# The order of 512- and 256-column matmuls inside the wide block products of two gated FFNs

## The chip, the cores and the metric

The kernel is one program on one core of a Trainium2 chip. The metric is the device time of one execution in microseconds (us), taken as the median over several runs. Matrix products run on TensorE (PE in the profile; its weight loads stand in a row of their own, PEld), sums and evacuations on VectorE (DVE), copies and activations on ScalarE (ACT), a few sums and some DMA issues on GpSimd (POOL), and most loads are issued by SyncE (SP).

## The reference, cut to what matters

The kernel computes a two-layer decoder trunk over 512 tokens of width 1024 in float32. Each layer adds a mixer to the residual stream and then a gated feed-forward network (FFN) of inner width 2816; a final norm ends it. The change touches the two FFNs alone:

```
def gated_conv_ffn(x, w_gate, w_up, conv_w, conv_b, w_down):
    g = jnp.einsum('bsd,df->bsf', x, w_gate)
    g = causal_dwconv3(g, conv_w) + conv_b
    up = jnp.einsum('bsd,df->bsf', x, w_up)
    return jnp.einsum('bsf,fd->bsd', jax.nn.silu(g) * up, w_down)
...
    hn = rms_norm(h, norm_ffn[layer])
    h = h + gated_conv_ffn(hn, w_ffn_gate[layer], w_ffn_up[layer], ...)
```

## The kernel before, in words

**Split floats.** TensorE multiplies in a format that keeps only part of a float32, so every operand is split into a high part (`hi`, a rounded copy made by ACT) and a low part (`lo`, the remainder, made by DVE or by an accumulating DMA that POOL issues). A product is then hi·hi + hi·lo + lo·hi. In most of the kernel this is three matmuls per 128 rows of the contraction (`mm3`, L157 to L159): the same high weights against the high and the low moving operand, then the low weights against the high moving operand.

**FFN by units.** The 22 blocks of 128 inner columns are worked off in units of two, `f` = 0, 2, ... 20, once in each layer. Unit 0 is computed directly. Each of the other ten is a fast block product (seven half-size products in place of eight) for the gate (`g`) and for the up projection (`u`): 14 products a unit, in the order written in `Ffn.products`. Each product contracts 512 rows, that is `NP` = 4 steps `kp`, with stationary weights of 128 columns and half the tokens (`HALF` = 256) as the moving operand. Between the units stand the down projections (`d` in layer 0, `dn` in layer 1) through `mm3`, long runs of 512-column matmuls.

**One block product** is the function `multiply` (L558 to L583). It has two forms:

- Narrow (`both` is None, L577 to L583): for each `kp` three 256-column matmuls into the first half of one PSUM bank.
- Wide (`both` given, L569 to L576): the tiles of the moving operand hold hi and lo side by side, so one 512-column matmul takes the high weights against both (hi·hi into columns 0 to 255 of the bank, hi·lo into columns 256 to 511), and a 256-column matmul adds lo·hi onto the first half. The wide form first runs the four 512-column matmuls of `kp` = 0 to 3 (L571), then the four 256-column ones (L574). `start` is set only on the first matmul into a freshly opened bank, so the order of the others doesn't matter to the sum. DVE adds both halves of the bank afterwards (`add`, L804).

`in_both` chooses the form: all products of units 6 to 20 are wide; in unit 4 all seven of the gate and three of the up projection are; in unit 2 none is.

**What sets the order.** A scheduler orders the instructions of each engine, with the program's order as its guide; tiles come from rotating pools (`whi` and `wlo`, six buffers each; seven PSUM banks `mm`), and a tile's next writer waits for its last reader. Some instructions are tied to others by hand (`behind`, `inorder`). The last matmul that `multiply` issues is kept in `last_matmul` and is what the fetch of the second layer's parameters is tied behind.

**Weights of a unit** (`prepare`): four loads by SP, then sums (`s12`, `s34`) on DVE and splits on ACT with DVE or with POOL's accumulating DMA. Names in the profile: `whi_a`/`wlo_a`, `whi_s12g`, `wlo_s34u` and so on; `g_20b` is a PSUM bank of unit 20's gate.

Of the kernel before, what the change touches and what calls it, by code (L numbers as in the profile page):

```python
# [31 lines left out]
def tile_trunk(ctx: ExitStack, tc: tile.TileContext, x, norm_mix, norm_ffn, final_norm,  # L32
# [13 lines left out]
    def mm_bank(name):  # L46
        return ps_mm.tile([P, 512], F32, tag="mm", name=name)
# [501 lines left out]
    NP = NK // 2  # L549
# [8 lines left out]
    def multiply(banks, name, product, left, right, both=None):  # L558

        at = BANK[product]
        first = at not in banks
        if first:
            banks[at] = mm_bank(f"{name}{at}")
        ps = banks[at][:, :HALF]
        if both is not None:  # L569
            for kp in range(NP):  # L570
                nc.tensor.matmul(banks[at], left(kp)[0], both(kp), start=first and kp == 0,  # L571
                                 stop=kp == NP - 1, skip_group_check=True)
            for kp in range(NP):
                last_matmul[0] = nc.tensor.matmul(ps, left(kp)[1], right(kp)[0], start=False,  # L574
                                                  stop=kp == NP - 1, skip_group_check=True)
            return banks[at]  # L576
        for kp in range(NP):  # L577
            (a_hi, a_lo), (b_hi, b_lo) = left(kp), right(kp)
            for l, r, end in ((a_hi, b_hi, False), (a_hi, b_lo, False),
                              (a_lo, b_hi, kp == NP - 1)):  # L580
                nc.tensor.matmul(ps, l, r, start=first, stop=end, skip_group_check=True)  # L581
                first = False
        return ps  # L583
# [8 lines left out]
    class Ffn:  # L592
# [127 lines left out]
        def multiply(self, banks, name, product, weights_, both):  # L720
            hi, lo = weights_
            return multiply(banks, name, product, lambda kp: (hi[:, kp, :], lo[:, kp, :]),
                            lambda kp: self.moving(product, kp),
                            (lambda kp: self.moving_both(product, kp)) if both else None)
# [173 lines left out]
    def mixer1(norm):  # L898
        w = w_in_odd[0]
        with tc.tile_pool(name="m1", bufs=1) as mp:  # L900
# [72 lines left out]
            class InProducts:  # L973
# [31 lines left out]
                def run(self, out_, done, behind_first):  # L1005
                    banks = ({}, {})
                    e = {}
                    for i, product in ((0, 1), (1, 1), (0, 2), (1, 2), (0, 6), (1, 6), (0, 5),
                                       (0, 7), (1, 5), (1, 7), (0, 4), (0, 3), (1, 4), (1, 3)):
                        if (i, product) == (0, 2):  # L1010
                            behind_first()
                        hi, lo = self.stat[product]
                        ps = multiply(banks[i], f"{self.name}_{i}", product, tokens(product, i),
                                      lambda kp: (hi[:, kp, :], lo[:, kp, :]))
                        c = {1: (0, 0), 2: (0, 0), 6: (0, 1), 3: (0, 1), 7: (1, 1), 5: (1, 1),
                             4: (1, 0)}[product]
                        dst = out_(i + 2 * c[0])[:, c[1] * HALF : (c[1] + 1) * HALF]
                        if product in (1, 6):
                            nc.scalar.copy(dst, ps)
                        elif product == 5:  # L1020
                            e[i] = ps
                        elif product == 7:
                            nc.scalar.copy(dst, ps)
                            nc.vector.tensor_tensor(dst, e[i], dst, ALU.add)
                            gelu(dst, dst, i + 2)
                        elif product == 4:
                            gelu(dst, ps, i + 2)
                            done(i + 2)
                        else:
                            nc.vector.tensor_tensor(dst, ps, dst, ALU.add)  # L1030
                        if product == 3:
                            row = out_(i)
                            gelu(row, row, i)
                            done(i)
# [398 lines left out]
```

## Time and profile before

| | |
|---|---|
| median of 3 runs (lowest to highest) | 975.62 us (975.47 to 975.7) |
| span of the profiled execution, first to last instruction | 973.0 us |
| PE busy | 963.6 us, 99%, 5120 matmuls |
| DVE busy | 817.0 us, 84% |
| ACT busy | 598.7 us, 62% |
| 512-column matmuls of the wide products (L571) | 976 |
| 256-column matmuls of the wide products (L574) | 976 |
| 256-column matmuls of the narrow products (L581) | 768 |

The profile is of one execution. Its own device time is not listed apart from its span; the span and the median differ by 2.6 us. A matmul's row carries its start, its modelled duration, its line and its tiles (`out<-in`, then the shape of the output). Matmuls overlap in the rows: the next one starts long before the duration of the one before has ended, so the pace is read from the distance of the starts. The timeline merges neighbours of the same line and tiles into one row (x4): the first start, and the time from it to the end of the last. Since matmuls overlap in the rows, the busy share of PE says little here.

### The profile page before, as it was taken

How to read it: one execution, taken by the hardware profiler on the slowest of the kernel's cores; microseconds unless marked ns; L12 is line 12 of the kernel's file. 1: busy time of each engine (PE TensorE's matmuls, PEld its weight loads, DVE VectorE, ACT ScalarE, POOL GpSimd, SP SyncE). 2: the span in 40 equal slices, each digit the busy share in tenths (PEclk: the TensorE clock that was granted, in tenths of full speed). 3: DMA queues.
4: the chain of work that ended last, by engine and by line, in shares of the span. 5: the costliest groups of instructions: out<-in, count | busy, mean ns of one | idle time of the engine just before them, and what ended most of it. 6: DMA issues, size and time to landing. Idle time of an engine off the chain costs nothing.

```text
span 973.0 us, 14003 instructions
## 1 busy us (share of the span) xinstructions
PE 963.6 (99%) x5120; PEld 828.8 (85%) x5120; DVE 817.0 (84%) x1393; ACT 598.7 (62%) x905; POOL 149.9 (15%) x173
## 2 busy tenths in 40 slices
PE   9999999999999999999999999999999999999996
PEld 7888888988888888888889988889888888888885
DVE  5887458999899898998986865589998989889897
ACT  5523347765676665765487734587765667656775
POOL 2142023110111010110310001221111011100123
PEclk9999999999999999999999999999999999999999
DMA  7442225776777677774324623167767777668775
GB/s 251 146 139 86 87 88 108 178 178 165 195 178 181 146 178 185 174 174 140 119 58 110 221 67 99 55 132 187 186 145 194 196 173 172 156 165 201 194 153 140
DMA packets 94417, 148.36 MB, mean 152 GB/s; under 512 B 5156, under 2 KB 60428, under 8 KB 94348
## 3 DMA queue, kind: packets, MB, share of 16 engines
q1 hardware_dynamic: 78316, 98.69, 32.2%
q0 software_dynamic: 14256, 46.93, 26.7%
q10 hardware_dynamic: 1776, 1.84, 0.6%
q8 instruction: 40, 0.66, 0.3%
q14 instruction: 29, 0.24, 0.1%
HBM read 98.42 MB, written 2.10 MB: 103 GB/s over the span
## 4 chain that ended last, share of the span: by engine, by line
PE 99%; DVE 1%; issue 0%; ACT 0%; POOLq 0%; DVEq 0%; POOL 0%
PE dn L158 3%; PE d L158 3%; PE dn L159 3%; PE dn L157 3%; PE d L159 3%; PE d L157 3%; PE gu L157 2%; PE gu L159 2%; PE oo L159 1%; PE oo L157 1%; PE gu L158 1%; PE oe L157 1%; PE oe L159 1%; PE oo L158 1%; PE oe L158 1%; PE u_2a L581 1%
## 5 line engine op out<-in xcount | busy, mean ns | idle before, releaser
L617 DVE SCALAR_TENSOR_TENSOR c<-rows,prm,c 128x512 f32<-128x512 f32 x88 | 65.6, 748 | 1.5 <-ACT c L615 1.4
L144 POOL DMA_DIRECT2D wlo_g<-raw_g x20 | 17.2, 860 | 321.3 <-DVE kept L804 187.4
L158 PE MATMUL dn<-wlo_dn,a_hi 128*128 128x512 f32 x144 | 56.3, 391 | 0.0
L158 PE MATMUL d<-a_lo,whi_d 128*128 128x512 f32 x144 | 56.3, 391 | 0.0
L159 PE MATMUL dn<-whi_dn,a_lo 128*128 128x512 f32 x144 | 56.2, 391 | 0.0
L159 PE MATMUL d<-a_hi,wlo_d 128*128 128x512 f32 x144 | 56.2, 390 | 0.0
L157 PE MATMUL d<-a_hi,whi_d 128*128 128x512 f32 x144 | 56.2, 390 | 0.0
L157 PE MATMUL dn<-whi_dn,a_hi 128*128 128x512 f32 x144 | 56.2, 390 | 0.0
L731 ACT ACTIVATE whi_a<-raw_g 128x512 fp32r<-128x512 f32 x20 | 12.6, 631 | 61.0 <-PE g_10e L571 8.7
L213 POOL TENSOR_TENSOR ssq_f<-ssq_f,sq_f 128x512 f32<-128x512 f32 x14 | 19.8, 1411 | 134.4 <-ACT sq_f L212 99.5
L202 ACT ACTIVATE hg<-h,prm 128x512 fp32r<-128x512 f32 x24 | 17.3, 722 | 34.9 <-DVE h L315 34.9
L142 ACT ACTIVATE wlo_g<-raw_g 128x1024 fp32r<-128x1024 f32 x20 | 21.2, 1062 | 27.5 <-PE g_2e L581 8.8
L615 ACT ACTIVATE c<-rows,prm 128x512 f32<-128x512 f32 x44 | 31.3, 715 | 6.6 <-DVE rows L828 6.6
L1187 DVE SCALAR_TENSOR_TENSOR y<-dn,small,y 128x512 f32<-128x512 f32 x40 | 28.0, 749 | 8.6 <-PE dn L159 8.6
L625 ACT ACTIVATE s<-c,prm 128x512 f32<-128x512 f32 x44 | 31.4, 715 | 6.2 <-DVE c L617 6.1
L203 DVE SCALAR_TENSOR_TENSOR hg<-h,prm,hg 128x512 fp32r<-128x512 f32 x24 | 23.6, 986 | 11.1 <-ACT hg L202 11.1
L266 ACT ACTIVATE a_hi<-s 128x512 fp32r<-128x512 f32 x40 | 24.9, 627 | 11.4 <-PE d L159 7.7
L159 PEld LDWEIGHTS dn<-whi_dn,a_lo 128*128 128x128 f32 x144 | 27.1, 188 | 5.7
L159 PEld LDWEIGHTS d<-a_hi,wlo_d 128*128 128x128 f32 x144 | 27.1, 188 | 5.6
L153 DVE TENSOR_TENSOR wlo_dn<-raw_dn,whi_dn 128x1024 fp32r<-128x1024 f32 x18 | 22.0, 1224 | 11.7 <-ACT whi_dn L152 11.7
L157 PEld LDWEIGHTS dn<-whi_dn,a_hi 128*128 128x128 f32 x144 | 27.1, 188 | 5.3
L157 PEld LDWEIGHTS d<-a_hi,whi_d 128*128 128x128 f32 x144 | 27.1, 188 | 5.3
(1132 smaller groups left out, 3319.9 us busy)
## 6 DMA issues: line engine op xcount, KB each, us to landing
raw_g<-in_w_ffn_gate_dram SPq DMA_DIRECT2D x40, 512.0 KB, 3.8
raw_u<-in_w_ffn_up_dram SPq DMA_DIRECT2D x40, 512.0 KB, 4.0
raw_dn<-in_w_ffn_down_dram SPq DMA_DIRECT2D x22, 512.0 KB, 6.3
wlo_u<-raw_u POOLq DMA_DIRECT2D x21, 512.0 KB, 6.1
wlo_g<-raw_g POOLq DMA_DIRECT2D x20, 512.0 KB, 4.6
raw_d<-in_w_ffn_down_dram SPq DMA_DIRECT2D x18, 512.0 KB, 4.2
wlo_s12g<-s12g POOLq DMA_DIRECT2D x18, 512.0 KB, 6.3
wlo_s34g<-s34g POOLq DMA_DIRECT2D x18, 512.0 KB, 5.5
```

The lines of the kernel that those rows point to most:

```text
L142: first = nc.scalar.activation(lo, raw, AF.Copy, scale=-1.0)
L153: behind(nc.vector.tensor_tensor(lo, raw, hi.bitcast(F32), ALU.subtract), after[0])
L157: nc.tensor.matmul(ps, lhs[0], rhs[0], start=start, stop=False)
L158: nc.tensor.matmul(ps, lhs[0], rhs[1], start=False, stop=False)
L159: nc.tensor.matmul(ps, lhs[1], rhs[0], start=False, stop=stop)
L203: nc.vector.scalar_tensor_tensor(hg[k][1], h[k], g, hg[k][0].bitcast(F32), op0=ALU.mult, op1=ALU.subtract)
L213: nc.gpsimd.tensor_tensor(self.ssq, self.ssq, sq, ALU.add)
L266: nc.scalar.activation(hi, src, AF.Copy, scale=scale)
L615: nc.scalar.activation(c, t[:, 0:S], AF.Copy, scale=prm("cf", ft))
L617: self.last_conv = nc.vector.scalar_tensor_tensor(c, t[:, i : S + i], prm("cf", i * NF + ft), c, op0=ALU.mult, op1=ALU.add)
L625: self.last_silu = nc.scalar.activation(s, c, AF.Silu, bias=self.prm("bf", ft))
L1187: return nc.vector.scalar_tensor_tensor(dst, ps, ffn.cols[:, t : t + 1], dst, op0=ALU.mult, op1=ALU.add)
```

## The change

In the wide form, the second loop over `kp` goes: each 512-column matmul is followed at once by the 256-column matmul of the same `kp`. The number of instructions, their operands and shapes, the `start` and `stop` marks and the bank stay as they were.

```diff
         if both is not None:
             for kp in range(NP):
                 nc.tensor.matmul(banks[at], left(kp)[0], both(kp), start=first and kp == 0,
                                  stop=kp == NP - 1, skip_group_check=True)
-            for kp in range(NP):
                 last_matmul[0] = nc.tensor.matmul(ps, left(kp)[1], right(kp)[0], start=False,
                                                   stop=kp == NP - 1, skip_group_check=True)
             return banks[at]
```

The order of the built instructions, set beside that of before: on PE 732 of the 976 matmuls of L574 move (the fourth of each product stays last); the order of POOL and SP is the same in both; on DVE and ACT the scheduler exchanges neighbours in some units. In six products (`u_6b` of both layers, `u_8b`, `u_10b`, `u_14b` and `u_18b` of layer 0) it lets another product in between, before as after.

## The prediction

> **What bounds the kernel now.** I read the profile's page first, for the shares of the engines and the chain that ended last, then the waits of PE, then PE's timeline in the units that the change touches.
>
> ```profile
> span 973.0 us, 14003 instructions
> ...
> PE 963.6 (99%) x5120; PEld 828.8 (85%) x5120; DVE 817.0 (84%) x1393; ACT 598.7 (62%) x905; POOL 149.9 (15%) x173
> ...
> PEclk9999999999999999999999999999999999999999
> ...
> PE 99%; DVE 1%; issue 0%; ACT 0%; POOLq 0%; DVEq 0%; POOL 0%
> ```
>
> The chain is PE from end to end, at full granted clock. A busy PE could still be a waiting one, so the waits (line that waited <- who ended it: total us, times, longest):
>
> ```profile
> PE clock L61 <- DVE idle L56: 1.3, 1, 1.3
> PE z L441 <- ACT hg L409: 0.3, 1, 0.3
> ```
> ```profile
> PEld g_10a L571 <- DVE rows L804: 0.3, 1, 0.3
> ```
>
> In the FFNs PE's weight loader waits 0.3 us once, and nothing else. So what counts is the pace of the matmul stream itself: the distance from one start to the next. The change alters no instruction; it alters only which matmul stands next to which. How many are touched, from the stage sums taken by line over the whole span (busy us, count):
>
> ```profile
> 0.00:974.00 974.00, 266.15 (x976) 168.51 (x976) 1.00 0.60 152
> ```
> ```profile
> 0.00:974.00 974.00, 155.14 (x976) 149.55 (x976) 1.00 0.60 152
> ```
>
> The first is L571, the 512-column matmul (W below), the second L574, the 256-column one (N): 976 each, that is 244 wide products of WWWWNNNN, which become WNWNWNWN. 1 ns on a pair is 0.98 us on the kernel.
>
> **The paces that the trace shows.** Long runs of one size first: the down projection behind the last unit (all 512 columns), and unit 2 (all 256; each x2 row counts two):
>
> ```profile
> 937.87 0.39 PE L158 MATMUL dn<-wlo_dn,a_hi 128*128 128x512 f32 x1
> ...
> 945.58 0.39 PE L159 MATMUL dn<-whi_dn,a_lo 128*128 128x512 f32 x1
> ```
> ```profile
> 173.77 0.40 PE L581 MATMUL g_2a<-t,whi_s12g 128*128 128x256 f32 x2
> ...
> 185.29 0.40 PE L581 MATMUL g_2a<-t,whi_g 128*128 128x256 f32 x2
> ```
>
> The first fence spans 34 matmuls: 7.71 / 34 = 0.2268 us for a settled W. The second spans 8 products of 12: 11.52 / 96 = 0.1200 us for a settled N. A wide product at settled paces would be 4 x 0.2268 + 4 x 0.1200 = 1.387 us. Now the wide products themselves, first to last of unit 20, with the run of 512s that follows:
>
> ```profile
> 916.64 1.09 PE L571 MATMUL u_20a<-hg,whi_a 128*128 128x512 f32 x4
> 917.57 0.63 PE L574 MATMUL u_20a<-hg,wlo_a 128*128 128x256 f32 x4
> 918.04 1.09 PE L571 MATMUL g_20b<-hg,whi_g 128*128 128x512 f32 x4
> 918.97 0.64 PE L574 MATMUL g_20b<-hg,wlo_g 128*128 128x256 f32 x4
> ...
> 934.88 0.40 PE L157 MATMUL dn<-whi_dn,a_hi 128*128 128x512 f32 x1
> 935.11 0.40 PE L158 MATMUL dn<-wlo_dn,a_hi 128*128 128x512 f32 x1
> 935.35 0.40 PE L159 MATMUL dn<-whi_dn,a_lo 128*128 128x512 f32 x1
> 935.58 0.39 PE L157 MATMUL dn<-whi_dn,a_hi 128*128 128x512 f32 x1
> ```
>
> Thirteen products from 916.64 to 934.88: 18.24 / 13 = **1.403 us each**, 16 ns over the settled sum. Four W take 0.93 (0.2325 each, slower than settled), four N 0.47 (0.1175 each, faster than settled). And after N's, the W's of the down projection start 0.23 to 0.24 apart (935.11 to 935.58 is 0.47 for two) before they settle. So a W that follows N's is slower than one that follows many W's. The opposite case, a wide product right behind a run of 512s:
>
> ```profile
> 193.64 1.07 PE L571 MATMUL g_4a<-hg,whi_a 128*128 128x512 f32 x4
> ...
> 194.54 0.64 PE L574 MATMUL g_4a<-hg,wlo_a 128*128 128x256 f32 x4
> ```
>
> Four W in 0.90: settled pace. Hence neither the split moving tile nor the switch of line makes a W slow; what came before does.
>
> **The change part by part.** Nothing is removed or added; the terms are the W after an N and the N after a W, now four of each per product in place of one. Single matmuls in ns come from the rows of a line (count: min/median/max duration):
>
> ```profile
> L571 PE MATMUL g_4a<-hg,whi_a x8: 389/390/390, 193.6 to 676.9; 128*128 128x512 f32 x8
> ```
> ```profile
> L571 PE MATMUL g_4b<-hg,whi_g x1: 396/396/396, 196.5 to 196.5; 128*128 128x512 f32 x1
> ```
> ```profile
> L581 PE MATMUL u_4a<-hg,wlo_a x1: 284/284/284, 196.3 to 196.3; 128*128 128x256 f32 x1
> ```
> ```profile
> L571 PE MATMUL g_20b<-hg,whi_g x1: 396/396/396, 918.0 to 918.0; 128*128 128x512 f32 x1
> ```
> ```profile
> L574 PE MATMUL u_20a<-hg,wlo_a x2: 278/278/279, 917.8 to 917.9; 128*128 128x256 f32 x2
> ```
> ```profile
> L574 PE MATMUL g_4a<-hg,wlo_a x8: 278/283/284, 194.5 to 677.5; 128*128 128x256 f32 x8
> ```
>
> A duration is about 163 ns longer than the distance to the next start (390 in g_4a at a settled 226.8; 284 at the end of the narrow u_4a at a settled 120). The border of g_4b: the N before it 284 - 163 = 121, its first W 396 - 163 = 233, together 354. The border of g_20b: 278 - 163 = 115 and 233, together 348. I take the mean, **351 ns for a pair**, because it is the only place where the trace has an N and a W side by side in that order; the ends 348 and 354 are kept. A product becomes 4 x 0.351 = 1.404 against 1.403: +1 ns, x 244 = +0.2 us, with -2.7 us and +3.2 us at the ends (1.392 and 1.416).
>
> What moves with it: the first N of a product is now second in place of fifth, so its low weights are wanted three W's (0.70 us) earlier. The tightest that I found:
>
> ```profile
> 222.14 1.22 DVE L732 TENSOR_TENSOR wlo_s12u<-s12u,whi_s12u 128x1024 fp32r<-128x1024 f32 x1
> ```
> ```profile
> 225.38 0.28 PE L574 MATMUL u_6e<-t,wlo_s12u 128*128 128x256 f32 x1
> ```
>
> Written by 223.36, read at 225.38, then at about 224.7: 1.3 us are left; 0. The high weights are free later: the fourth W starts 3 x 0.351 = 1.05 us into the product, not 0.70. ACT waits for these buffers:
>
> ```profile
> ACT whi_a L731 <- PE g_10e L571: 8.7, 2, 4.5
> ```
>
> 4.5 us become about 4.9, on an engine that is idle 38% of the time: 0; if that cover were gone, twice 0.35 us in each of 18 units or 12.6 us, which bounds it. The product's last matmul, and with it the bank's evacuation, keeps its place. On DVE some neighbours change places, and DVE is close to full in these units:
>
> ```profile
> 320.00:500.00 180.00, 180.00 (x915) 153.38 (x914) 164.92 (x285) 111.38 (x159) 24.82 (x24) 1.00 0.60 152
> ```
>
> 164.92 / 180 = 92% of DVE. An add that frees a bank may come behind a 1.22 us split. I take two more waits of the size of the one listed (0.3 us), 0.6 us, and keep 18 of them, 5.4 us, as the upper end and 0 as the lower. DMAs keep their order on SP and POOL, so no transfer moves past another. **Sum:** +0.2 + 0.6 = +0.8 us on the span of 973.0; the span lies 2.6 us under the median of 975.62, and nothing touched lies outside it, so 975.6 + 0.8 = 976.4, said as 976.5.
>
> **The Trainium skill** (page "TensorE: Matmul & The Clock Gate", section "Back-to-back issue gap") gives the isolated distance of matmuls as columns / 2.4 + 2.5 ns, 215.8 and 109.2 here; the trace has 226.8 and 120.0, 11 ns more, and the measurement decides. By that rule a matmul's time hangs on its own size alone, which is the first rival below.
>
> **The rivals.**
> 1. *Blind to order.* Each matmul costs its size whatever stands beside it: the change is nothing, 975.6. Against it: W at 0.225 in g_4a and 0.2325 elsewhere. 0.08.
> 2. *The switch has a fee (slower).* The 16 ns that a product pays over the settled sum are the price of one round from W to N and back; four rounds pay four times: 3 x 16 = 48 ns x 244 = +11.7 us, 987; three fees in place of four if part of it is shared, 984. It decides from 2 ns a round more than now. For it: the excess is there in every product behind another, and missing where a product follows 512s. Against it: it builds up over several W's (0.93 for four), so one W should pay a part. 0.20.
> 3. *Short runs never upset the pace (faster).* The slow W's come from a run of N's; a single N leaves the settled pace alone. Pair 226.8 + 120.0: 1.387, -16 ns x 244 = -3.9 us, 971.7; 0.16. If the lone N also keeps the short distance of the first N behind a settled run (278 - 163 = 115), 1.367: -8.8 us, 966.8; 0.05. Against it: at both borders above the very first W is slow already.
> 4. *Engines fall behind.* The exchanged adds on DVE make PE wait as in the upper end: +5.4 us, 981. Against it: one wait in 244 products today. 0.11.
>
> That the change doesn't do what it says is excluded but for six products, between whose matmuls the scheduler lets another product, as before.
>
> **How the numbers follow.** The forecast (pair at 348 to 354) has 0.40: 0.04 of it faster, 0.24 the same, 0.12 slower, by 0.2% or 1.95 us, about what a measurement of this kernel can tell from no change. Rival 1 adds 0.08 to the same, rival 2 0.20 to slower, rival 3 0.21 to faster, rival 4 0.09 to slower and 0.02 to the same. Faster 0.25, same 0.34, slower 0.41. The likeliest case alone gives 973 to 979. For 8 in 10 the range goes down to 971, which leaves out rival 3's second price, and up to 986, which leaves out the upper half of rival 2.
>
> **What would show it.** In the profile after, the rows of L571 and L574 stand singly, so each start can be read. A pair of 0.348 to 0.354 and products of 1.39 to 1.42 bear out the forecast; 0.347 or less is rival 3; 0.36 and more is rival 2. PE waits on DVE's L804 of over 2 us in total are rival 4. ACT's wait for L571 should grow by 0.35 us each, at no cost. Wrong I would be above all if an N alone between two W's sets a pace that no row of before shows.

## The result, and the profile after

| | before | after |
|---|---|---|
| median of 7 runs (lowest to highest) | 975.25 us (975.03 to 975.7) | 977.65 us (977.21 to 979.59) |
| span of the profiled execution | 973.0 us | 975.5 us |

The change costs 2.4 us: a ratio of 1.0029, with a 95% interval of 1.0018 to 1.004. That is slower by 0.2 to 0.3%. The forecast was 976.5, in a range of 971 to 986.

The page of the kernel after, its span, its engines and its chain:

```profile
span 975.5 us, 14004 instructions
...
PE 965.6 (99%) x5120; PEld 826.8 (85%) x5120; DVE 815.9 (84%) x1393; ACT 597.7 (61%) x905; POOL 150.4 (15%) x173
...
PE 97%; ACT 1%; DMA 1%; DVE 1%; issue 0%; POOLq 0%; DVEq 0%; POOL 0%
```

The busy shares say almost nothing. The chain says something: before, it was PE at 99% and DVE at 1%. DVE's 1%, the work at the end, is still there; new is that the chain leaves PE between 210 and 226 us, for ACT and then for one DMA. So there is a new wait. The waits of PE's weight loader in the kernel after (who waited, for whom: total us, times, longest; the lines of `multiply` and `add` have moved up by one, L573 for L574, L803 for L804):

```profile
PEld u_6b L573 <- DMA wlo_u<-raw_u: 0.7, 1, 0.7
...
PEld g_16a L571 <- DVE rows L803: 0.3, 2, 0.2
PEld g_12a L571 <- DVE rows L803: 0.3, 2, 0.2
```

**Where the time lies.** The stretch from the first wide product of a layer to the down projection behind the last unit holds all that the change touches. In layer 1, PE's timeline of after, then of before:

```profile
677.20 0.39 PE L571 MATMUL g_4a<-hg,whi_a 128*128 128x512 f32 x1
...
948.27 0.39 PE L1280 MATMUL dn_a<-whi_dnp,hg 128*128 128x512 f32 x1
```
```profile
676.25 0.62 PE L571 MATMUL g_4a<-hg,whi_a 128*128 128x512 f32 x2
...
945.80 0.39 PE L1281 MATMUL dn_a<-whi_dnp,hg 128*128 128x512 f32 x1
```

271.07 us against 269.55. The same was worked out for both layers and for two traces of each kernel (the second ones are the first and the ninth experiment). From the starts of all matmuls of the wide products I took the mean distance to the next start, W and N added to a pair. A W with more than 245 ns to the next start, or an N with more than 130, was counted as a wait, with what it has over 235 or 118 ns:

| | stretch, layer 0 / 1 (us) | pair (ns) | waits (us) |
|---|---|---|---|
| before | 269.75 / 269.55 | 350.17 / 350.28 | 0.26 / 0.00 |
| before, second trace | 270.19 / 269.55 | 350.15 / 350.28 | 0.72 / 0.00 |
| after | 271.56 / 271.08 | 352.25 / 351.63 | 1.08 / 0.90 |
| after, second trace | 271.47 / 271.58 | 352.13 / 352.44 | 1.03 / 0.89 |

Everything else in the program has kept its length, but for the start-up (the time to the first product of unit 2) and the mixer of the second layer, which differ by 0.8 and 0.6 us between the two traces of after as well. The start-up is why the two spans lie only 2.5 us apart: it took 167.24 us in the first trace of after, 168.02 in that of before. The stretches give +3.3 us in these traces (542.85 against 539.52 for both layers together, the means of two traces). Of this the pace is 1.9 ns x 976 = 1.85 us, and the waits are 1.95 - 0.5 = 1.45 us. **Two halves**, and either could be the whole in a theory; the experiments take them apart.

**The first new wait, one of 0.66 us.** PE's timeline of after, at the product that the scheduler splits:

```profile
225.13 0.28 PE L573 MATMUL u_6e<-t,wlo_s12u 128*128 128x256 f32 x1
225.25 0.40 PE L571 MATMUL u_6b<-hg,whi_u 128*128 128x512 f32 x1
226.04 0.39 PE L573 MATMUL u_6b<-hg,wlo_u 128*128 128x256 f32 x1 [0.40 <-DMA wlo_u<-raw_u]
226.27 0.39 PE L571 MATMUL u_6b<-hg,whi_u 128*128 128x512 f32 x1
```

The tile `wlo_u` of after (the DMA that makes it, its first and last start, then its time to landing), and before the first W's of `u_6b` and the N's that read the tile:

```profile
L144 POOL DMA_DIRECT2D wlo_u<-raw_u x1: 859/859/859, 218.3 to 218.3; - x1
...
DMA to landing us min/median/max: 7.7/7.7/7.7
```
```profile
225.86 0.86 PE L571 MATMUL u_6b<-hg,whi_u 128*128 128x512 f32 x3
```
```profile
L574 PE MATMUL u_6b<-hg,wlo_u x4: 281/282/284, 231.0 to 231.4; 128*128 128x256 f32 x4
```

The low weights land at 218.3 + 7.7 = 226.0. Before, they landed at 219.0 + 7.6 = 226.6, and the first of the N's stood at 231.0: the scheduler had let three whole products in between the first W of `u_6b` (225.86) and its N's. Now the first N is the second matmul of `u_6b`, due at 225.25 + 0.24 = 225.49.

**The other new waits, 18 of 0.01 to 0.10 us in the distances of starts, together 1.3.** They all stand at the first W of product 7 (on `s34g` or `s34u`), which writes the bank that product 6 has left to DVE. Unit 12 of layer 0, before: ACT, DVE, PE.

```profile
317.46 1.06 ACT L152 ACTIVATE whi_d<-raw_d 128x1024 fp32r<-128x1024 f32 x1 [0.55 <-PE g_12a L571]
318.42 0.35 ACT L816 COPY rows<-g_12a 128x256 f32<-128x256 f32 x1
```
```profile
318.55 1.23 DVE L153 TENSOR_TENSOR wlo_d<-raw_d,whi_d 128x1024 fp32r<-128x1024 f32 x1 [1.17 <-ACT whi_d L152]
319.69 0.42 DVE L804 TENSOR_TENSOR rows<-g_12a,rows 128x256 f32<-128x256 f32 x1
```
```profile
320.49 1.09 PE L571 MATMUL g_12a<-t,whi_s34g 128*128 128x512 f32 x4
```

And after, the same three engines:

```profile
318.05 1.06 ACT L152 ACTIVATE whi_d<-raw_d 128x1024 fp32r<-128x1024 f32 x1 [0.91 <-PE g_12a L571]
319.01 0.35 ACT L815 COPY rows<-g_12a 128x256 f32<-128x256 f32 x1
```
```profile
319.14 1.23 DVE L153 TENSOR_TENSOR wlo_d<-raw_d,whi_d 128x1024 fp32r<-128x1024 f32 x1 [1.16 <-ACT whi_d L152]
320.28 0.42 DVE L803 TENSOR_TENSOR rows<-g_12a,rows 128x256 f32<-128x256 f32 x1
```
```profile
320.63 0.28 PE L573 MATMUL u_12a<-t,wlo_s12u 128*128 128x256 f32 x1
320.76 0.50 PE L571 MATMUL g_12a<-t,whi_s34g 128*128 128x512 f32 x1
```

Read it as a chain. ACT's next instruction, the copy of the down projection's high weights (`whi_d`), needs the buffer that product 6's high weights leave, and these are read by the fourth W. The brackets show ACT's wait grown from 0.55 to 0.91 us. DVE's `wlo_d` needs `whi_d`, and behind it on DVE stands the add that frees the bank. The add starts 0.59 us later than before (320.28 for 319.69), while PE itself is only 0.27 us later (320.76 for 320.49). Before, the add had ended 0.38 us ahead of the W (319.69 + 0.42 = 320.11); now 0.06 us (320.70), and that is too little: the W's row is 0.50 long in place of 0.40, and the next start comes 0.33 us after its own.

### The profile page after: what moved, and what is told of

Read it like the earlier page. It is cut to its first block, busy times and chain, and to the rows that moved or that the text cites. A ratio compares the mean times of both kernels' runs of the same rounds, so it can differ in the third digit from the quotient of the medians.

```text
span 975.5 us, 14004 instructions
## 1 busy us (share of the span) xinstructions
PE 965.6 (99%) x5120; PEld 826.8 (85%) x5120; DVE 815.9 (84%) x1393; ACT 597.7 (61%) x905; POOL 150.4 (15%) x173
## 4 chain that ended last, share of the span: by engine, by line
PE 97%; ACT 1%; DMA 1%; DVE 1%; issue 0%; POOLq 0%; DVEq 0%; POOL 0%
PE dn L159 3%; PE dn L158 3%; PE dn L157 3%; PE d L157 3%; PE d L159 3%; PE d L158 3%; PE gu L157 2%; PE gu L159 1%; PE oo L159 1%; PE oo L158 1%; PE gu L158 1%; PE oe L159 1%; PE oe L157 1%; PE oo L157 1%; PE oe L158 1%; PE u_2a L580 1%
## 5 line engine op out<-in xcount | busy, mean ns | idle before, releaser
L730 ACT ACTIVATE whi_a<-raw_g 128x512 fp32r<-128x512 f32 x20 | 12.6, 632 | 62.0 <-PE g_8e L571 8.8
L158 PEld LDWEIGHTS dn<-wlo_dn,a_hi 128*128 128x128 f32 x144 | 27.1, 188 | 5.4
L158 PEld LDWEIGHTS d<-a_lo,whi_d 128*128 128x128 f32 x144 | 27.1, 188 | 5.3
```

Source lines behind the costliest of these rows:

```text
L158: nc.tensor.matmul(ps, lhs[0], rhs[1], start=False, stop=False)
```

## The experiments

**Theory A**: the two halves are separate and add up, a slower pace of the order 1+1 and waits that come from product 6's weights being freed late and from `u_6b`. **Rivals**: B, each switch between W and N has a fee of its own; C, the waits are all, and the slower pairs only their echo; D and E, on the pace, that it suffers only at the switches, or that the first two N's are cheap and the later ones dear. F, G and H came up later.

All kernels but those of e1 and e9, which are after and before unchanged, share one edit: the two lines in the loop become a loop over a string that gives the order of the product's matmuls (W and N, each in the order of `kp`).

```diff
+            for kind in ORDER:
+                kp, seen[kind] = seen[kind], seen[kind] + 1
...
```

Only ORDER is shown below; after is `"WNWNWNWN"`, before `"WWWWNNNN"`. Each time stands beside its own runs of before: 974.82 for the first four, 974.94 for the next four, 974.91 and 974.85 for the last two pairs.

| run | time (us) | ratio to before, 95% | stretch 0 / 1 (us) | pair (ns) | waits (us) |
|---|---|---|---|---|---|
| e1 after again | 977.99 | 1.0035 (1.0023 to 1.0048) | 271.47 / 271.58 | 352.13 / 352.44 | 1.03 / 0.89 |
| e2 product 6 grouped | 977.79 | 1.0032 (1.0021 to 1.0042) | 271.70 / 270.69 | 351.27 / 352.28 | 1.68 / 0.00 |
| e3 only product 6 split | 975.89 | 1.0011 (1.0002 to 1.002) | 269.95 / 270.38 | 349.74 / 349.73 | 0.65 / 1.13 |
| e4 2+2 | 972.92 | 0.9981 (0.9972 to 0.999) | 269.74 / 268.63 | 348.31 / 348.29 | 1.35 / 0.28 |
| e5 pace alone | 976.78 | 1.0017 (1.0008 to 1.0026) | 271.44 / 270.65 | 351.69 / 352.21 | 1.14 / 0.00 |
| e6 only `u_6b` grouped | 977.41 | 1.0022 (1.0013 to 1.0032) | 270.52 / 271.27 | 351.19 / 352.08 | 0.56 / 0.91 |
| e7 runs of eight | 973.39 | 0.9986 (0.9977 to 0.9995) | 270.03 / 268.65 | 349.14 / 349.10 | 1.33 / 0.00 |
| e8 2+2, three places 4+4 | 972.81 | 0.9979 (0.997 to 0.9987) | 269.59 / 268.52 | 348.47 / 348.45 | 1.08 / 0.00 |
| e9 before again | 975.39 | one run | 270.19 / 269.55 | 350.15 / 350.28 | 0.72 / 0.00 |
| e10 3+3, 1+1 | 975.78 | 1.0012 (1.0002 to 1.0021) | 270.25 / 270.45 | 350.25 / 350.20 | 0.77 / 1.02 |
| e11 1+1 with turned pairs | 978.76 | 1.0043 (1.0026 to 1.006) | 271.60 / 271.41 | 351.64 / 352.66 | 1.48 / 0.90 |
| e12 the same without waits | 975.19 | 1.0007 (0.9998 to 1.0017) | 269.73 / 270.15 | 350.48 / 351.58 | 0.23 / 0.20 |

**e1**, the kernel after once more, as the ground for the others.

> The changed kernel once more, beside the others of this group. Theory A (two halves: a pace of 352 ns a pair in place of 350.2, +1.75 us, and new waits of PE, +1.65 us, that come from high weights freed 0.35 us later and from low weights wanted earlier): +2 to +3 us, and the waits of the first profile stand at the same places (first W of product 7 behind unit 12, 16, 20; the second matmul of u_6b). Rival B (the switch between sizes has a fee, 0.8 us for each further round in a product; waits only take up what PE would lose elsewhere): +2 to +3 us, waits anywhere. Rival C (waits alone, no pace): +2 to +3 us, and the pairs that do not wait stand 350 ns apart.

It repeats the result: +3.2 us here, both halves as in the first trace.

**e2** gives product 6 its old order, so its high weights are free as early as before:

```diff
-ORDER = "WNWNWNWN"
+ORDER = "WWWWNNNN" if product == 6 else "WNWNWNWN"
```

> As changed, but product 6 of gate and up goes back to 4+4 (36 of 244 products), so that its high weights are freed early again. A: the waits before product 7 go (about -1.0 us) and 36 products get their pace back (-0.25 us): +1.1 to +1.5 us over before, and the first W of s34g and s34u takes 230 to 240 ns in every unit. B: 36/244 of 2.4 us less: +2.0 us. C: +1.4 us.

In layer 1 the waits go from 0.90 to 0.00, and what is left of the stretch, 270.69 - 269.55 = 1.14 us, is pace alone (352.28 - 350.28 = 2.0 ns x 488 pairs = 0.98). So the chain through product 6's weights is what makes those waits, and C falls: the pairs stay slow without a wait. The time hardly moved, +3.0 us over before where A had +1.1 to +1.5, since in this trace layer 0 lost elsewhere what it had gained. PE's loader in this run:

```profile
PEld u_6b L578 <- DMA wlo_u<-raw_u: 0.8, 1, 0.8
PEld u_10a L575 <- DVE kept L809: 0.7, 1, 0.7
```

**e3** is the mirror image, before with product 6 alone at 1+1:

```diff
-ORDER = "WWWWNNNN"
+ORDER = "WNWNWNWN" if product == 6 else "WWWWNNNN"
```

> As before, but product 6 of gate and up alone is 1+1 (36 of 244 products). A: the waits before product 7 come back alone, +1.0 us, with a pace of +0.25 us: +1.0 to +1.3 us; no wait at u_6b. B: 36/244 of 2.4 us: +0.35 us. C: +1.0 us.

Layer 1 gets 1.13 us of waits in 15 places from this one product, with the pairs no slower than before. The wait half by itself costs 1.07 us.

**e4** doubles the switches of before instead of making four times as many:

```diff
-ORDER = "WNWNWNWN"
+ORDER = "WWNNWWNN"
```

> Every wide product as WWNNWWNN: two rounds of sizes in place of one or four. The fourth W starts 0.93 us into the product, 0.23 us later than before (0.35 in the changed kernel), which is less than the 0.38 us that the bank was free ahead of product 7. A: no waits before product 7, some at u_6b, pace between the two: +0.5 to +1.3 us. B: one further round, +0.8 us. C: +0.4 us, from u_6b alone.

Faster than before, by 1.9 us, at 348.3 ns a pair and with PE's loader still waiting 1.3 us at `u_6b`. A fee per switch (B) would put two rounds between one and four; they lie below both. B falls. A had put the pace between the two as well, and missed it.

**e5** keeps 1+1 wherever no new wait hangs on it:

```diff
-ORDER = "WNWNWNWN"
+ORDER = ("WWWWNNNN" if product == 6 or product == 2 and name in ("u0_6", "u1_6")
+         else "WNWNWNWN")
```

> 1+1 everywhere but in product 6 of gate and up and in product 2 of up in unit 6, which are 4+4: 206 products changed, the three places that waited taken out. Theory A (pace and waits are separate costs and add up): no wait before product 7 nor at u_6b, pairs at 352, and the two FFN stretches longer by 2 ns x 824 = 1.6 us together; time +1.4 to +2.0 us. Rival C (waits alone): +0.0 to +0.3 us. Rival B (fee for each switch) is the same as A here and has fallen with WWNNWWNN, which was faster than before.

Layer 1 has no wait and a pair of 352.2; layer 0 has only waits in places where the second trace of before has some as well (`g_10a`, `u_10a`, `u_18a`). 1.8 us over before is left, the size of the pace half (1.73 ns x 976 = 1.7 us). The waits of layer 0 differ by 0.4 us or more from trace to trace of one kernel, so the cleaner proof is layer 1: 270.65 - 269.55 = 1.1 us longer, without a wait.

**e6** groups `u_6b` alone:

```diff
-ORDER = "WNWNWNWN"
+ORDER = ("WWWWNNNN" if product == 2 and name in ("u0_6", "u1_6")
+         else "WNWNWNWN")
```

> 1+1 everywhere but in product 2 of up in unit 6, which is 4+4. A: the wait of 0.6 to 0.8 us on the low weights that a DMA still writes is gone from layer 0, the waits before product 7 stay: layer 0's stretch about 270.8, layer 1's 271.1 to 271.6, time +2.4 us. If that wait only takes the place of another one right behind it: 271.5 in layer 0, +3 us as for the changed kernel.

Layer 0's waits fall from 1.03 to 0.56 us, layer 1's stay (0.91). The interval of the total overlaps those of e1 and e5, so it is the trace that shows the effect: the wait at `u_6b` is gone.

**e7** makes runs of eight, by turning every other product round:

```diff
-ORDER = "WWWWNNNN"
+ORDER = "WWWWNNNN" or "NNNNWWWW" in turn
```

> Every second wide product begins with its four narrow matmuls (NNNNWWWW), so that equal sizes stand in runs of eight: half the switches of before. Theory D (the pace suffers only at switches and then settles): a pair at 348.5 to 349, -1.2 to -1.8 us. Theory E (it is not the switches: the first two narrow matmuls behind wide ones are the cheap ones at 115 to 117, the third and later cost 119 to 120, and wide ones behind any narrow run cost 232 to 235): a pair at 350 to 351, 0 to +0.7 us, and waits on top because the high weights of every second product are freed 0.47 us later.

Half the switches of before, 1.1 ns a pair less and 1.55 us faster. This is near what D named, and E falls. But the pairs of runs of two are shorter still, though they have more switches than before, so the number of switches doesn't order the paces, and D falls as a rule too: 352.1, 348.3, 350.2 and 349.1 ns for runs of one, two, four and eight. In units 6 to 20 product 6 falls on the 4+4 turns, so this run says nothing on the waits before product 7. The 1.33 us of layer 0 stand almost all at one place, `g_10a`.

**e8** is the version that the results so far pointed to:

```diff
-ORDER = "WNWNWNWN"
+ORDER = ("WWWWNNNN" if product == 6 or product == 2 and name in ("u0_6", "u1_6")
+         else "WWNNWWNN")
```

> WWNNWWNN, but product 6 of gate and up and product 2 of up in unit 6 at 4+4. A: the pace of WWNNWWNN (348.3 a pair) in 206 products and none of its waits (1.35 us in layer 0, 0.28 in layer 1 there): stretches of 268.9 and 268.7, time -1.6 to -2.4 us. If the waits do not add up with the pace: no better than WWNNWWNN everywhere, -1.2 to -1.9 us.

972.81 beats both kernels, before by 2.1 us; against e4 the difference is within the intervals. Layer 1 came out as expected. Layer 0 did not: the wait at `u_6b` is gone, but layer 0 has 1.08 us of others, almost all at `g_10a` and `u_18a`, where the second trace of before waits as well, so its stretch is 269.59 and not 268.9. Its page and PE's timeline in unit 20:

```profile
span 972.0 us, 14002 instructions
```
```profile
914.36 0.62 PE L576 MATMUL g_20a<-hg,whi_a 128*128 128x512 f32 x2
...
918.53 0.63 PE L576 MATMUL g_20e<-t,whi_s12g 128*128 128x512 f32 x2
```

Three products in 4.17 us, 1.390 each, against 1.403 before.

**e9** is before once more, for the spread between traces.

> The kernel before, unchanged, for a second trace of it: how far do two traces of one kernel lie apart in the mean distance of a pair? Two traces of the kernel after gave 352.25 and 352.13 ns in layer 0, 351.63 and 352.44 in layer 1. Theory A (the pace hangs on the lengths of the runs of equal size, which is the same in every execution) expects 350.2 +- 0.5 in both layers and at most 5 waits. A rival that the paces differ from execution to execution, and not with the order, expects a layer at 351.5 or more, or at 348.5 or less.

The pairs of before agree to 0.02 ns; the waits of layer 0 are what differs (seven matmuls in five places now, four in three in the first trace). So the pace of 4+4 belongs to the order. That of 1+1 does so less strictly: in layer 1 the two traces of after lie 0.8 ns apart, for a reason that the last section shows.

**e10** has as many switches as e4, but in runs of three and of one:

```diff
-ORDER = "WNWNWNWN"
+ORDER = "WWWNNNWN"
```

> WWWNNNWN in every product: two switches to N a product, as in the order 2+2, but of runs of three and of one. Theory A with paces by the place in the run (W behind N 233 to 235, second W 234, third 228 to 232; first N 115 to 117, the others 119) expects a pair near 351.0 ns, so +0.8 ns against 4+4, +0.8 us on 976 pairs, and waits about as after (up to 1.7 us): 975.5 to 977.5. Rival F, that the pace hangs on the number of switches alone, expects the 348.3 ns of 2+2: about 973.

350.2 ns: F falls, and my own sum by the place in the run (351.0) is 0.8 off; that the time lies within 975.5 to 977.5 even so is luck. Pace as before and waits of 1.8 us, where the two traces of before have 0.3 and 0.7: another look at the wait half alone, +0.9 us.

**e11 and e12** came out of the distances in ns, product by product (last section): the order 1+1 has a slow and a fast rhythm. Could a turned pair bring the stream into the fast one?

```diff
-ORDER = "WNWNWNWN"
+ORDER = "WNWNWNNW" if product in (1, 7) else "WNWNWNWN"
```

> The order 1+1, but with the last pair of products 1 and 7 turned round (WNWNWNNW), so that twice in each half-unit two N and then two W stand side by side. Theory G: a stream of single W and N has two rhythms, a slow one that repeats every three pairs (W 241, 236, 233 and N 120, 113, 117 ns: 353 a pair) and a fast one (W 230, N 117: 346.7 a pair); in the kernel after each unit begins in the slow one, and in units 10, 14 and 18 of layer 0, behind a place where two N stand side by side, it changes to the fast one for five products. So the turned pairs should bring most products into the fast rhythm: a mean pair of 347.5 to 349.5 ns, the waits as after (1.5 to 2.2 us): 973 to 975. Rival H, the rhythm does not come from such a place, but from chance or from waits: 351.5 to 352.5 ns as after, 977 to 978.5.

No: in most units the products behind a turned pair stay at 351 to 355 ns. Over to the fast rhythm go units 10, 14 and 18 of layer 0, as in the kernel after, and unit 6 of layer 0, behind the wait at `u_6b`. The run is the slowest of all. G as I had put it falls. e12 adds the cure for the waits:

```diff
+ORDER = ("WNWNWNNW" if product in (1, 7) else "WNWNWWNN" if product == 6
+         else "WWWWNNNN" if product == 2 and name in ("u0_6", "u1_6") else "WNWNWNWN")
```

> As the run before, and product 6 as WNWNWWNN, whose high weights are free about 0.11 us sooner than in 1+1, and the two u_6b products at 4+4. The waits of product 7 in the kernel after are 0.06 to 0.10 us each, so they should go: waits in layer 1 at most 0.3 us, 0.3 to 1.0 in layer 0. If theory G holds (347.5 to 349.5 ns a pair): 972 to 973.5, about the time of the order 2+2. If not (352): 976.5 to 977.

Most of the waits went (0.23 and 0.20 us are left): moving the fourth W up by one N, 0.12 us, is most of what the chain needs, though in unit 12 the first W of product 7 still takes 292 ns in layer 0 and 286 in layer 1, some 0.05 us over the 235 counted as no wait. The pace stayed near the slow one. Its time is that of before (0.9998 to 1.0017), below the 976.5 to 977 that I had named for this case: the two products that follow product 6 of the gate run at 346 to 348 ns in nearly every unit, which I hadn't foreseen (last section).

## Why the prediction came out as it did

- **PE bounds the kernel and the distances of starts are what to count**: right. What the change cost lies in the two stretches.
- **A pair of 348 to 354 ns, taken as 351**: right in its bounds, short in the value. It is 352.1 (the mean of two traces), so the first term of the sum, +0.2 us, was +1.85 us. The mean of two borders was no measure: the distances go through a repeating pattern, and two samples of it say which values occur, not how often. So with the N's of before, read as 0.1175 us each and faster than settled: that is one kind of product, and in turn with it four N's take 478 ns, 119.5 each. The prediction's last sign of being wrong came true in part as well: a W between single N's takes up to 241 ns, and without a wait no W of the wide products takes over 237 in the first trace of before.
- **"The tightest that I found" for the low weights**: wrong step. The search took products that stand in one piece. `u_6b`, named in the same text as split by the scheduler, was the one whose N's moved by 5.5 us (231.0 to 225.5) and not by 0.7. Cost 0.66 us, put at 0.
- **"0, ACT idle 38%" for the high weights**: wrong step, and the one that taught most. The wait grew as predicted (0.55 to 0.91 us, 0.36 for 0.35), but ACT's share of idle time was no cover. What counts is what is queued behind the waiting instruction and who waits for that: `whi_d`, then DVE's `wlo_d`, then the add behind it, then PE's bank. Slack of 0.38 us was used up to 0.06. It cost 1.3 us in 18 places, far under the bound of 12.6, since the slack took most of the delay.
- **Exchanged neighbours on DVE, +0.6 us**: waits of PE on DVE's L803 did come, 1.3 us in all, but for another reason; that a term of this kind stood in the sum at all is luck. In unit 12 DVE's add stands behind the same split before and after; it is the split that comes late.
- **The sum**: +0.8 forecast, +2.4 measured, +3.3 in the traces' stretches. It lies in the forecast's upper part, which had 0.12 of the 0.40, and on the side that had the largest chance, slower at 0.41. But half of that chance came from rival 2, whose mechanism fell. That the time lies in the range is no proof of the working: 971 to 986 is wide enough for rival 1, for the first price of rival 3 and for rival 4 as well.
- **Rival 1, blind to order**: refuted by the pairs of 348.3 to 352.1 ns for the same 976 W's and N's. The isolated gap of the Trainium skill (page "TensorE: Matmul & The Clock Gate", section "Back-to-back issue gap") depends on a matmul's columns alone; by that formula all orders would take the same. The traces don't agree, and they decide.
- **Rival 2, the fee**: refuted by e4, two rounds a product and yet a shorter pair than before (348.3 ns for 350.2), and by e10, two rounds at the pace of one (350.2); e7 alone would have fitted it. **Rival 4**: of its kind, but 1.3 us in place of 5.4.
- **Rival 3, short runs keep the settled pace, 346.8**: refuted as the rule, but not absurd: 37 of the 238 products that stand in one piece run at just that, 346 to 347 ns, in the first trace of after (27 in the second).

## What to carry to other kernels

When a step makes a buffer free later, follow the instruction that waits for it on its engine, then what is queued behind it there, and then who needs that; an idle share of the engine is no cover. When an order is changed inside a product, look first at the products that the scheduler has split, since there an instruction may move by microseconds. And where two orders of the same matmuls are equally legal, measure several (here runs of two beat runs of one and of four; against eight the shorter pair shows in the traces alone, for the intervals of the times overlap): the pace of short patterns was not to be had from the pace of long ones.

## What the runs showed of the hardware

The pace of a steady stream of matmuls isn't a sum of a price for each. At full granted clock (1.00 in both stretches below) and without a wait the distances of starts go through repeating patterns, and the mean depends on which pattern it is. PE's timeline of after has both of its patterns in one unit, unit 18 of layer 1; first the slow one, three products:

```profile
889.56 0.40 PE L571 MATMUL g_18b<-hg,whi_g 128*128 128x512 f32 x1
...
893.80 0.40 PE L571 MATMUL u_18e<-t,whi_s12u 128*128 128x512 f32 x1
```
```profile
900.97 0.39 PE L571 MATMUL g_18e<-hg,whi_s34g 128*128 128x512 f32 x1
...
905.13 0.39 PE L571 MATMUL u_18a<-t,whi_u 128*128 128x512 f32 x1
```

4.24 us for twelve pairs, then 4.16: 353 and 347 ns a pair with the same order, shapes and weights' sizes. The distances of starts in ns, worked out from the trace (for 1+1 in pairs of a W and an N, for 4+4 four W's and then four N's):

```
1+1, slow: 241 120 | 236 113 | 233 117 | 241 120 | ...     1060 for three pairs, 353.3
1+1, fast: 230 117 | 230 116 | 230 117 | ...               346.7
      or:  231 112 | 233 117 | 231 112 | ...               346.5
4+4:       235 233 236 224  118 120 120 120  and  233 236 229 232  117 120 117 117   in turn, 351.5 and 350.2
settled:   226.8 for W in a long run, 120.0 for N: 346.8 for the two
```

Every unit of after begins in the slow pattern, in both traces; in layer 0 units 10, 14 and 18 go over to the fast one (the second form) behind a product that the scheduler has split, in layer 1 some units do behind a wait, and not the same ones in both traces, which is where the 0.8 ns between them come from. The order in runs of two (e4) stays at 348 ns in most products. What makes the stream fall into one pattern or the other is not settled: switches don't order it, e11 shows that a turned last pair (two N's, then two W's across the border) doesn't bring it about by itself, and the start of the weight load doesn't move with it (within 5 ns of the matmul before the one it serves in both patterns). One order did bring it about reliably: in e12 the 1+1 product right behind product 6 of the gate, which ends in WWNN there, runs at 346.5 or 346.75 ns a pair in all 16 units where one stands there; behind the 4+4 product 6 of e5 it is 347.75 or 348.0 in 14 of 16. Why is open. If all 976 pairs ran in the fast pattern, the kernel would be 3.5 ns x 976 = 3.4 us under before; no run here reached that.
